# The FFN's down projection as seven-product block multiplications

## The chip, the cores and the metric

The kernel runs on one core of one Trainium2 chip. The metric is the device time of one execution in microseconds (us). The five engines are called as in the profile: PE (matrix multiply; PEld is its weight load), DVE (vector), ACT (scalar), POOL (GpSimd) and SP (which here only issues DMA transfers).

## What is computed

One layer of an encoder for 1024 prompt tokens and 64 sample tokens, 1088 in all, with 1024 channels. The change lies in its last part, the SwiGLU feed-forward network (FFN) with 2816 hidden channels:

```
xn2 = rms_norm(x, lw["norm_ffn_g"])
f = (jax.nn.silu(xn2 @ lw["w_ffn_gate"]) * (xn2 @ lw["w_ffn_up"])) @ lw["w_ffn_down"]
x = x + f
```

The products before it (attention, a recurrent branch, memory attention, three branch projections, one output projection) are not changed.

## The kernel before

**Numbers in two parts.** Every matrix operand is split into a high part (a cast on ACT, line 72) and a low part (a subtraction on DVE, line 73). A product is three matmuls: high by high, high by low, low by high. Activations lie with channels on the 128 partitions and the 1088 tokens along the free dimension, so a "block" of 128 channels is a 128 x 1088 tile.

**The plain form.** `down` (line 1210 and on) takes one block of 128 output channels at a time. For each of three token chunks (364, 364, 360) it accumulates over the contraction blocks of a group, three matmuls each (`mm3`, lines 101 to 103), into one PSUM bank; DVE then adds the bank to the output tile (line 1229). The 22 hidden blocks are taken in groups of 8, 8 and 6, and within each group all 8 output blocks: 24 calls.

**The seven-product form.** The branch projections, the output projection, gate and up already use `sw_product` (line 202). It takes a pair of output blocks at a time and pairs of contraction blocks, and the tokens in two halves of 544, so that each pair is a 2 x 2 by 2 x 2 block product, done with seven products in place of eight. `PAIRS` (line 168) lists the seven with their operands in the order in which PE does them: A11, S3, S2, A22, S1, A12, S4 on the weight side and B11, T3, T2, T4, T1, B21, B22 on the activation side. For each of the seven PE does two column pieces of 272, and for each piece all contraction pairs, three matmuls each (line 212). The first three products are copied out of PSUM by ACT (line 218), because later results need them as well; the others are evacuated by the caller's `out` on DVE and POOL.

`sw_weights` (line 170) loads the weights of one such step (two transfers of 512 KB on SP), forms the four combinations S1 to S4 on DVE and splits all seven operands on ACT and DVE. The steps run one ahead: while PE does one, the next one's weights are made. For the branch outputs the activation side comes from DRAM: `put_branch` (line 293) stores three blocks as they are, forms T3, T1, T2, T4 on POOL in place (lines 299 to 302) and stores those; `load_operands` (line 996) loads 28 operands of 272 KB, seven for each of four contraction pairs, and splits each into the place from `operand_at` (line 993). A place is free once PE has done the earlier product with the operand that lies there.

**Gate, up and down.** For each of 11 pairs of hidden blocks, `gate_pair` and `up_pair` do a gate and an up step. The results are scaled per token on POOL (line 1169), gate goes through SiLU on ACT (line 1178), and DVE multiplies them (line 1185). `up_pair` then stores the two hidden blocks whole to DRAM (`hid_scr`, line 1187). For the down projection `load_h` (line 1203) loads them back, 544 KB each, in the order of need, and splits them. The down weights come through `load_w` on ACT's DMA queue. The last group's finished output blocks are transposed on PE (line 1244), copied by ACT (line 1246) and written out, while the next block is being computed.

A scheduler of the framework puts the instructions of each engine in order when the kernel is built. Each engine, and SP's queue, then works in that order, and an instruction that waits holds up all behind it on its engine.

Of the kernel before, what the change touches and what calls it, by code (L numbers as in the profile page):

```python
# [9 lines left out]
F32 = mybir.dt.float32  # L10
# [39 lines left out]
def kernel(ctx: ExitStack, tc: tile.TileContext, x_prompt, x_sample, mem_prompt, cache_sb_k, cache_sb_v,  # L50
# [16 lines left out]
    def f32(t):  # L67
        return t.bitcast(F32)

    def split(h, l, src, h_eng=None, l_eng=None):  # L70

        (h_eng or S.copy)(h, src)  # L72
        (l_eng or V).tensor_sub(l, src, f32(h))  # L73
# [216 lines left out]
    o_scr = [{o: [drm.tile([P, HT], F32, name=f"o{b}{o}{i}") for i in range(KT // 2)] for _, o in PAIRS}  # L290
             for b in range(3)]

    def put_branch(b, i, x0, x1):

        d = o_scr[b]
        x0l, x0h, x1l, x1h = x0[:, :HT], x0[:, HT:], x1[:, :HT], x1[:, HT:]
        for o, src in (("B22", x1h), ("B11", x0l), ("B21", x1l)):
            ST.dma_start(d[o][i], src)
        G.tensor_sub(x1h, x1h, x0h)
        G.tensor_sub(x0h, x0h, x0l)  # L300
        G.tensor_add(x0l, x0l, x1h)
        G.tensor_sub(x1l, x1l, x0l)
        for o, src in (("T3", x1h), ("T1", x0h), ("T2", x0l), ("T4", x1l)):
            ST.dma_start(d[o][i], src)

    def o_tile(name):
        return wpl.tile([P, T], F32, tag="wx", name=name, bufs=3)
# [629 lines left out]
    if True:  # L937
# [4 lines left out]
        NI = KT // 2  # L942
        LO, HI = slice(0, HT), slice(HT, T)
        x1_scr = [drm.tile([P, T], F32, name=f"x1_{k}") for k in range(KT)]
        hid_scr = [drm.tile([P, T], F32, name=f"hid{k}") for k in range(FFN // P)]


        UNITS = [(act, f"A{x}{k}") for k in range(KT) for x in "hl"] + [(bp, f"B{k}") for k in range(16)]
# [3 lines left out]
        def at(place, name, dt=F32R):  # L952
            return place[0].tile([P, T], dt, tag=place[1], name=name, bufs=RAWB if place is RAW else 1)
# [19 lines left out]
        def pair_weights(src, j, nm):  # L973
            return sw_weights(src[0, :, 2 * j * P:2 * (j + 1) * P], f"{nm}{j}", w_slot, w_stage)
# [21 lines left out]
        def load_operands(b):  # L996
            X = {o: [] for _, o in PAIRS}
            for oi, (_, o) in enumerate(PAIRS):
                for i in range(NI):
                    t = operand_at(oi, i, f"x{b}{o}{i}")  # L1000
                    ST.dma_start(f32(t[:, 1]), o_scr[b][o][i])
                    split(t[:, 0], t[:, 1], f32(t[:, 1]))
                    X[o].append(t)
            return X

        def form_operands(xs, temps, nm):

# [44 lines left out]

        br_w = (w_br_sb, w_br_lru, w_br_mem)
        W = pair_weights(w_br_sb, 0, "wb0")
        X = load_operands(0)
        for b in range(3):
            for j in range(NI):
                if j + 1 < NI:
                    Wn = pair_weights(br_w[b], j + 1, f"wb{b}")
                elif b < 2:  # L1060
                    Wn = pair_weights(br_w[b + 1], 0, f"wb{b + 1}")
                else:
                    Wn = pair_weights(w_out, 0, "wo")
                branch_pair(b, j, W, X)
                W = Wn
            if b < 2:
                X = load_operands(b + 1)
# [114 lines left out]
        def up_pair(j, W, sil):  # L1182
            u = [at(cycle("u", U_PLACES), f"u{j}{f}", F32) for f in range(2)]
            sw_product(W, XS, NI, banks4, temp,
                       ffn_out(u, lambda f, hf, c, d: V.tensor_mul(d, d, sil[f][:, piece(hf, c)])))  # L1185
            for f in range(2):
                ST.dma_start(hid_scr[2 * j + f], u[f])

        for j in range(NH // 2):
            Wn = pair_weights(w_ffn_up, j, "fu")  # L1190
            sil = gate_pair(j, W)
            W = pair_weights(w_ffn_gate, j + 1, "fg") if j + 1 < NH // 2 else None
            up_pair(j, Wn, sil)


        groups = [list(range(0, 8)), list(range(8, 16)), list(range(16, 22))]
        Hh, Hl = {}, {}

        def load_h(j):
            q = 2 * (j % 16)  # L1200
            Hh[j] = at(UNITS[q], f"hh{j}")
            Hl[j] = at(UNITS[q + 1], f"hl{j}")
            ST.dma_start(f32(Hl[j]), hid_scr[j])
            split(Hh[j], Hl[j], f32(Hl[j]))

        def load_x1(f):
            mg[f] = mgp.tile([P, T], F32, tag=f"mg{f}", name=f"y{f}")
            ST.dma_start(mg[f], x1_scr[f])
# [11 lines left out]
        for j in groups[0]:  # L1220
            load_h(j)
        mg = [None] * KT
        load_x1(0)
        for gi, js in enumerate(groups):
            fin = gi == len(groups) - 1
            Xg = ([Hh[j] for j in js], [Hl[j] for j in js])
            for f in range(KT):
                def ev(s, n, p):
                    V.tensor_add(mg[f][:, s:s + n], mg[f][:, s:s + n], p)  # L1229

                if gi == 0:
                    load_h(8 + f)
                    if f + 1 < KT:
                        load_x1(f + 1)
                w = load_w(w_ffn_down[0, js[0] * P:(js[-1] + 1) * P, f * P:(f + 1) * P], f"fd{gi}{f}", nk=len(js))
                down(w, Xg, ev, len(js))
                if fin:
                    for g in range(3):
                        m = 4 if g < 2 else 1
                        n = P if g < 2 else DSEQ  # L1240
                        p = ps.tile([P, 512], F32, tag="tr", name="ytp", bufs=2)
                        for q in range(m):
                            t = 4 * g + q
                            TE.transpose(p[:n, q * P:(q + 1) * P], mg[f][:, t * P:t * P + n], ident)  # L1244
                        yt = at(SPARE[g], "yt", F32)
                        S.copy(yt[:n, :m * P], p[:n, :m * P])
                        fs = slice(f * P, (f + 1) * P)
                        if g < 2:
                            ST.dma_start(y_prompt[0, g * 512:(g + 1) * 512, fs].rearrange("(t p) n -> p t n", p=P),
                                              yt[:, :512].rearrange("p (t n) -> p t n", n=P))  # L1250
                        else:
                            ST.dma_start(y_sample[0, :, fs], yt[:n, :P])
            if gi == 0:
                for j in groups[2]:
                    load_h(j)
# [32 lines left out]
```

## Time and profile before

| what | us |
|---|---|
| median of 3 runs (2421.33 to 2422.0) | 2421.39 |
| the profiled execution's own time | 2413.88 |
| its span, first to last instruction | 2412.1 |
| PE busy in the span | 2324.9 |
| DVE busy | 1346.5 |
| ACT busy | 1027.7 |
| POOL busy | 623.8 |
| mean granted PE clock, share of full | 0.989 |

The spans below are counted from the first instruction. Gate and up run from about 1650 to 2127, the down projection from there to the end. In the timeline a row merges instructions of one kind: its start, the time that it covers, the engine, the line, the tiles written and read, a count, and in brackets the idle time before it and what ended it. A matmul's own duration includes the flow through the array, so the distance between starts says what one costs in a stream.

### The profile page before, as it was taken

How to read it: one execution, taken by the hardware profiler on the slowest of the kernel's cores; microseconds unless marked ns; L12 is line 12 of the kernel's file. 1: busy time of each engine (PE TensorE's matmuls, PEld its weight loads, DVE VectorE, ACT ScalarE, POOL GpSimd, SP SyncE). 2: the span in 40 equal slices, each digit the busy share in tenths (PEclk: the TensorE clock that was granted, in tenths of full speed). 3: DMA queues.
4: the chain of work that ended last, by engine and by line, in shares of the span. 5: the costliest groups of instructions: out<-in, count | busy, mean ns of one | idle time of the engine just before them, and what ended most of it. 6: DMA issues, size and time to landing. Idle time of an engine off the chain costs nothing.

```text
span 2412.1 us, 39508 instructions
## 1 busy us (share of the span) xinstructions
PE 2324.9 (96%) x15941; PEld 2271.5 (94%) x15941; DVE 1346.5 (56%) x2248; ACT 1027.7 (43%) x1968; POOL 623.8 (26%) x657
## 2 busy tenths in 40 slices
PE   7999999999999999999999999798999999999999
PEld 6899999989999999999998998698999999989998
DVE  4666666665555554334466876769565656562322
ACT  5555555553534533323354653465433343330211
POOL 3223232321222221111113365624322222210000
PEclk9999999999999999999999999898999999999999
DMA  4112121213233233222255662142222222261222
GB/s 145 56 51 69 51 76 52 76 56 109 81 118 105 81 121 106 83 96 90 83 189 174 215 231 91 54 156 85 77 83 72 83 71 90 77 242 59 83 58 63
DMA packets 254221, 238.87 MB, mean 99 GB/s; under 512 B 11331, under 2 KB 217366, under 8 KB 254038
## 3 DMA queue, kind: packets, MB, share of 16 engines
q1 hardware_dynamic: 132184, 172.30, 21.3%
q10 hardware_dynamic: 121854, 64.05, 9.1%
q8 instruction: 125, 2.05, 0.4%
q14 instruction: 58, 0.48, 0.1%
HBM read 167.32 MB, written 68.98 MB: 98 GB/s over the span
## 4 chain that ended last, share of the span: by engine, by line
PE 64%; POOL 5%; DVE 3%; issue 2%; DMA 2%; ACT 2%; SPq 0%; ACTq 0%; POOLq 0%; DVEq 0%
PE sw L212 24%; PE mm L103 11%; PE mm L101 11%; PE mm L102 11%; POOL swt L1045 2%; POOL mg L1049 2%; DMA sig<-g 1%; PE mmk L101 1%; PE mmk L102 1%; PE mmk L103 1%; PE ytp L1244 0%; DVE xgT L73 0%; PE gt L103 0%; PE gt L101 0%; PE gt L102 0%
## 5 line engine op out<-in xcount | busy, mean ns | idle before, releaser
L218 ACT COPY swt<-sw 128x272 f32<-128x272 f32 x228 | 86.8, 386 | 137.2 <-PE sw L212 132.1
L1229 DVE TENSOR_TENSOR y<-y,mm 128x364 f32<-128x364 f32 (+1 forms) x72 | 38.3, 531 | 181.6 <-PE mm L103 181.6
L1169 POOL TENSOR_TENSOR u<-u,R 128x272 f32<-128x272 f32 x66 | 66.5, 1009 | 180.8 <-DVE u L1168 180.8
L460 DVE TENSOR_TENSOR_SCAN e<-ones,e 128x128 f32<-128x128 f32 (+3 forms) x64 | 97.0, 1525 | 0.8
L277 DVE TENSOR_SCALAR gst<-mm,prm 128x364 f32<-128x364 f32 (+1 forms) x72 | 42.6, 592 | 98.3 <-PE mm L103 98.0
L1169 POOL TENSOR_TENSOR sil<-sil,R 128x272 f32<-128x272 f32 x66 | 51.2, 779 | 140.8 <-DVE sil L1168 139.3
L459 DVE SCALAR_TENSOR_TENSOR e<-z,e 128x384 f32<-128x384 f32 (+4 forms) x96 | 50.4, 552 | 61.2 <-ACT e L457 57.6
L464 ACT ACTIVATE e<-e 128x128 f32<-128x128 f32 (+3 forms) x64 | 43.8, 685 | 60.0 <-DVE e L463 52.2
L1185 DVE TENSOR_TENSOR u<-u,sil 128x272 f32<-128x272 f32 x88 | 40.3, 461 | 47.2 <-POOL u L1169 46.5
L1045 POOL TENSOR_TENSOR swt<-swt,sig 128x272 f32<-128x272 f32 x48 | 49.2, 1024 | 66.3 <-DVE swt L1044 45.7
L1178 ACT ACTIVATE sil<-sil 128x272 f32<-128x272 f32 x88 | 37.5, 431 | 61.9 <-POOL sil L1169 57.2
L73 DVE TENSOR_TENSOR al<-at,ah 128x128 fp32r<-128x128 f32 (+2 forms) x96 | 51.1, 547 | 20.5 <-ACT ah L72 20.5
L1049 POOL TENSOR_TENSOR mg<-mg,swt 128x272 f32<-128x272 f32 x64 | 60.6, 956 | 5.5 <-DVE swt L1047 1.8
L748 POOL TENSOR_TENSOR ig<-ig,xc 128x1092 f32<-128x1092 f32 x8 | 20.4, 2554 | 129.2 <-ACT ig L740 129.2
L1038 ACT ACTIVATE sig<-sig 128x544 f32<-128x544 f32 x48 | 31.3, 662 | 50.7 <-DMA sig<-g 40.9
L101 PE MATMUL z<-kh,qh 128*128 128x384 f32 (+4 forms) x96 | 36.6, 381 | 14.6 <-DVE e L463 14.6
L455 ACT ACTIVATE e<-z 128x384 f32<-128x384 f32 (+4 forms) x96 | 45.7, 484 | 10.6 <-PE z L103 7.7
L463 DVE TENSOR_TENSOR e<-z,e 128x384 f32<-128x384 f32 (+4 forms) x96 | 48.9, 542 | 0.0
L820 POOL TENSOR_TENSOR sq<-sq,sqt 128x364 f32<-128x364 f32 (+1 forms) x12 | 13.6, 1131 | 133.1 <-ACT sqt L819 133.1
L72 ACT CAST ah<-at 128x128 fp32r<-128x128 f32 (+2 forms) x96 | 43.0, 471 | 10.1 <-PE at L512 10.1
L102 PE MATMUL av<-al,vh 128*128 128x256 f32 x160 | 46.7, 292 | 0.2
L101 PE MATMUL av<-ah,vh 128*128 128x256 f32 x160 | 46.4, 290 | 0.4 <-ACT ah L72 0.4
(1813 smaller groups left out, 8492.2 us busy)
## 6 DMA issues: line engine op xcount, KB each, us to landing
sig<-g SPq DMA_DIRECT2D x48, 272.0 KB
hid<-u SPq DMA_DIRECT2D x22, 544.0 KB
hl<-hid SPq DMA_DIRECT2D x22, 544.0 KB
g<-gst SPq DMA_DIRECT2D x48, 182.0 KB
out_dram<-kvs SPq DMA_DIRECT2D x32, 256.0 KB
o0T<-oh SPq DMA_DIRECT2D x16, 272.0 KB
o1T<-ol SPq DMA_DIRECT2D x16, 272.0 KB
o2T<-om SPq DMA_DIRECT2D x16, 272.0 KB
```

The source lines that it names most:

```text
L73: (l_eng or V).tensor_sub(l, src, f32(h))
L101: TE.matmul(out, lh, rh, start=start, stop=False)
L102: TE.matmul(out, lh, rl, start=False, stop=False)
L103: TE.matmul(out, ll, rh, start=False, stop=stop)
L212: TE.matmul(bank[c][:, :HC], w[:, wj, i], x[:, xj, cs], start=start and i == 0 and j == 0, stop=i == n - 1 and j == 2, skip_group_check=True)
L218: S.copy(tmp[c][:, j], bank[c][:, :HC])
L459: V.scalar_tensor_tensor(ev, z, 0.0, ev, op0=ALU.max, op1=ALU.add)
L460: V.tensor_tensor_scan(e[:, ::-1], ones1[:n].to_broadcast([n, L]), e[:, ::-1], 0.0, op0=ALU.mult, op1=ALU.add)
L463: V.tensor_sub(ev, z, ev)
L1045: G.tensor_mul(t if b else d, t, g)
L1049: G.tensor_add(d, d, t)
L1169: G.tensor_mul(d, d, r)
```

## The change

`up_pair` no longer stores the hidden blocks whole. It calls `put_operands`, which is the body of `put_branch` with the destination given, so that each pair leaves seven block operands of 272 KB in DRAM. `load_operands` takes a list of such sets. The down projection runs through `sw_weights`, `load_operands` and `sw_product` in 12 steps: three groups of 4, 4 and 3 contraction pairs, four pairs of output blocks in each. At each group's beginning 28 (at the last 21) operands are loaded into the places that the step before is still using. The first step's weights are made during the last up step, and all down weights now come on SP's queue. DVE evacuates each step with two additions in place of one where a kept product is needed; for the last pair of output blocks the second is on POOL. In the last group, the outputs of a step are transposed and written after the next step is issued, with their copies in the pool that also holds the kept products (`raw`, three buffers).

```diff
-    def put_branch(b, i, x0, x1):
-
-        d = o_scr[b]
+    def put_operands(d, x0, x1):
+
         x0l, x0h, x1l, x1h = x0[:, :HT], x0[:, HT:], x1[:, :HT], x1[:, HT:]
         for o, src in (("B22", x1h), ("B11", x0l), ("B21", x1l)):
-            ST.dma_start(d[o][i], src)
+            ST.dma_start(d[o], src)
         G.tensor_sub(x1h, x1h, x0h)
         G.tensor_sub(x0h, x0h, x0l)
         G.tensor_add(x0l, x0l, x1h)
         G.tensor_sub(x1l, x1l, x0l)
         for o, src in (("T3", x1h), ("T1", x0h), ("T2", x0l), ("T4", x1l)):
-            ST.dma_start(d[o][i], src)
+            ST.dma_start(d[o], src)
...
-        hid_scr = [drm.tile([P, T], F32, name=f"hid{k}") for k in range(FFN // P)]
+        h_scr = [{o: drm.tile([P, HT], F32, name=f"h{o}{i}") for _, o in PAIRS} for i in range(FFN // P // 2)]
...
-            for f in range(2):
-                ST.dma_start(hid_scr[2 * j + f], u[f])
+            put_operands(h_scr[j], *u)
+
+        groups = [range(0, 4), range(4, 8), range(8, 11)]
...
-            W = pair_weights(w_ffn_gate, j + 1, "fg") if j + 1 < NH // 2 else None
+            W = pair_weights(w_ffn_gate, j + 1, "fg") if j + 1 < NH // 2 else down_weights(0, 0)
...
-        def down(w, X, evac, nk):
-            wh, wl = w
-            for ci, (s, n) in enumerate(CH):
-                pool, tag = BANKS[ci]
-                p = pool.tile([P, 512], F32, tag=tag, name="mm", bufs=2)
-                for k in range(nk):
-                    mm3(p[:, :n], wh[:, k, :], wl[:, k, :], X[0][k][:, s:s + n], X[1][k][:, s:s + n],
-                        k == 0, k == nk - 1)
-                evac(s, n, p[:, :n])
...
+        def down_pair(gi, j, W, X):
+            def out(f, hf, c, p, t, add):
+                d = mg[2 * j + f][:, piece(hf, c)]
+                if add:
+                    V.tensor_add(t, p, t)
+                    (G if j == NI - 1 else V).tensor_add(d, d, t)
+                else:
+                    V.tensor_add(d, d, p)
...
+            sw_product(W, X, len(groups[gi]), banks4, temp, out)
...
-                        yt = at(SPARE[g], "yt", F32)
+                yt = at(RAW, "yt", F32) if g < 2 else half("yt")
...
+        for q, (gi, j) in enumerate(steps):
+            if j == 0:
+                X = load_operands([h_scr[i] for i in groups[gi]], f"h{gi}")
+            Wn = down_weights(*steps[q + 1]) if q + 1 < len(steps) else None
+            down_pair(gi, j, W, X)
+            W = Wn
+            if gi == len(groups) - 1 and j > 0:
+                y_out(2 * j - 2)
+                y_out(2 * j - 1)
+        y_out(KT - 2)
+        y_out(KT - 1)
```

On POOL, between one up step and the next gate step, before (`u` is a hidden block, `sil` the gate's result, `R` the token scale):

```order
L1169 TENSOR_TENSOR u_20439<-u_20439,R_17275 128x272 x2
L1169 TENSOR_TENSOR sil_20679<-sil_20679,R_17275 128x272 x2
L1169 TENSOR_TENSOR sil_20679<-sil_20679,R_17276 128x272 x2
L1169 TENSOR_TENSOR sil_20678<-sil_20678,R_17275 128x272 x2
L1169 TENSOR_TENSOR u_20916<-u_20916,R_17275 128x272 x2
```

And on POOL at the same place now:

```order
L1176 TENSOR_TENSOR u_20548<-u_20548,R_17330 128x272 x2
L298 TENSOR_TENSOR u_20549<-u_20549,u_20548 128x544
L299 TENSOR_TENSOR u_20548<-u_20548 128x544
L300 TENSOR_TENSOR u_20548<-u_20548,u_20549 128x544
L301 TENSOR_TENSOR u_20549<-u_20549,u_20548 128x544
L1176 TENSOR_TENSOR sil_20797<-sil_20797,R_17330 128x272 x2
```

The four combinations stand between the up step's last scaling and the next gate step's first.

On SP, where the last up step passes into the down projection, before (`hl` is a hidden block loaded back, `y<-x` an output tile preset with the residual):

```order
L1203 DMA hl_22563<-hid_12603 128x1088
L1203 DMA hl_22654<-hid_12604 128x1088
L1187 DMA hid_12616<-u_22313 128x1088
L1203 DMA hl_22745<-hid_12605 128x1088
L1203 DMA hl_22836<-hid_12606 128x1088
L1187 DMA hid_12615<-u_22312 128x1088
L1203 DMA hl_22927<-hid_12607 128x1088
L1208 DMA y_22931<-x_5_12592 128x1088
```

And on SP at the same place now (`h0B`, `h0T` are the first group's operands; `hB`, `hT` on the left are the last pair's stores):

```order
L1005 DMA h0B_22789<-hB_12607 128x544
L1005 DMA h0B_22793<-hB_12614 128x544
L303 DMA hT_12666<-u_22489 128x544
L303 DMA hT_12669<-u_22488 128x544
L303 DMA hT_12667<-u_22488 128x544
L303 DMA hT_12668<-u_22489 128x544
L1005 DMA h0B_22797<-hB_12621 128x544
L1005 DMA h0B_22801<-hB_12601 128x544
L1005 DMA h0B_22805<-hB_12608 128x544
L1005 DMA h0B_22809<-hB_12615 128x544
L1005 DMA h0B_22813<-hB_12622 128x544
L177 DMA fd01r_22817<-in_w_ffn_down_dram 128x4x256
```

Before, two stores stand among the loads there; now the last five loads of the first group (the last B21 and all four B22) stand behind the last pair's four T stores, which wait for POOL.

On DVE, where the first down step begins to be evacuated, before (`fd` are down weights, the last letter h or l the part):

```order
L73 TENSOR_TENSOR hl_23109<-hl_23109,hh_23108 128x1088
L73 TENSOR_TENSOR fd02l<-fd02r,fd02h 128x1024
L73 TENSOR_TENSOR hl_23200<-hl_23200,hh_23199 128x1088
L1229 TENSOR_TENSOR y_22567<-y_22567,mm 128x364 x2
L1229 TENSOR_TENSOR y_22567<-y_22567,mm 128x360
L73 TENSOR_TENSOR fd03l<-fd03r,fd03h 128x1024
L1229 TENSOR_TENSOR y_22658<-y_22658,mm 128x364 x2
```

And on DVE at that place now (`sw` is PSUM, `swt` a kept product):

```order
L1214 TENSOR_TENSOR swt<-sw,swt 128x272
L73 TENSOR_TENSOR h0B_22797<-h0B_22797 128x544
L1214 TENSOR_TENSOR swt<-sw,swt 128x272
L73 TENSOR_TENSOR h0B_22801<-h0B_22801 128x544
L1214 TENSOR_TENSOR swt<-sw,swt 128x272
L1215 TENSOR_TENSOR y_22850<-y_22850,swt 128x272 x2
L73 TENSOR_TENSOR h0B_22805<-h0B_22805 128x544
L1214 TENSOR_TENSOR swt<-sw,swt 128x272
L73 TENSOR_TENSOR h0B_22809<-h0B_22809 128x544
L1215 TENSOR_TENSOR y_22850<-y_22850,swt 128x272
L1214 TENSOR_TENSOR swt<-sw,swt 128x272
L73 TENSOR_TENSOR h0B_22813<-h0B_22813 128x544
```

The splits of the last loads stand between the evacuations of the first step, and each holds up those behind it.

More of the change, by code (lines that the diff above doesn't have):

```diff
@@ L303, in put_branch @@
         for o, src in (("T3", x1h), ("T1", x0h), ("T2", x0l), ("T4", x1l)):
-            ST.dma_start(d[o][i], src)
+            ST.dma_start(d[o], src)
+    def put_branch(b, i, x0, x1):
+        put_operands({o: o_scr[b][o][i] for _, o in PAIRS}, x0, x1)
     def o_tile(name):
@@ L994, in operand_at, with load_operands @@
             return at(UNITS[oi * NI + i], name).rearrange("p (x n) -> p x n", x=2)
-        def load_operands(b):
+        def load_operands(srcs, nm):
             X = {o: [] for _, o in PAIRS}
             for oi, (_, o) in enumerate(PAIRS):
-                for i in range(NI):
-                    t = operand_at(oi, i, f"x{b}{o}{i}")
-                    ST.dma_start(f32(t[:, 1]), o_scr[b][o][i])
+                for i, d in enumerate(srcs):
+                    t = operand_at(oi, i, f"{nm}{o}{i}")
+                    ST.dma_start(f32(t[:, 1]), d[o])
                     split(t[:, 0], t[:, 1], f32(t[:, 1]))
@@ L1004, in load_operands, with load_branch @@
             return X
+        def load_branch(b):
+            return load_operands([{o: o_scr[b][o][i] for _, o in PAIRS} for i in range(NI)], f"x{b}")
         def form_operands(xs, temps, nm):
@@ L1054 @@
         W = pair_weights(w_br_sb, 0, "wb0")
-        X = load_operands(0)
+        X = load_branch(0)
         for b in range(3):
@@ L1066 @@
             if b < 2:
-                X = load_operands(b + 1)
+                X = load_branch(b + 1)
         tt = [at(p, "tt", F32).rearrange("p (x n) -> p x n", x=2) for p in (RAW, SPARE[3])]
@@ L1185, in up_pair, with down_weights @@
                        ffn_out(u, lambda f, hf, c, d: V.tensor_mul(d, d, sil[f][:, piece(hf, c)])))
-            for f in range(2):
-                ST.dma_start(hid_scr[2 * j + f], u[f])
+            put_operands(h_scr[j], *u)
+        groups = [range(0, 4), range(4, 8), range(8, 11)]
+        mg = [None] * KT
+        def down_weights(gi, j):
+            r = groups[gi]
+            return sw_weights(w_ffn_down[0, 2 * r[0] * P:2 * (r[-1] + 1) * P, 2 * j * P:2 * (j + 1) * P],
+                              f"fd{gi}{j}", w_slot, w_stage)
         for j in range(NH // 2):
@@ L1191 @@
             sil = gate_pair(j, W)
-            W = pair_weights(w_ffn_gate, j + 1, "fg") if j + 1 < NH // 2 else None
+            W = pair_weights(w_ffn_gate, j + 1, "fg") if j + 1 < NH // 2 else down_weights(0, 0)
             up_pair(j, Wn, sil)
[L1196 to L1204, printed above, removed]
@@ L1206, in load_x1 @@
-        def load_x1(f):
-            mg[f] = mgp.tile([P, T], F32, tag=f"mg{f}", name=f"y{f}")
-            ST.dma_start(mg[f], x1_scr[f])
-        def down(w, X, evac, nk):
-            wh, wl = w
-            for ci, (s, n) in enumerate(CH):
-                pool, tag = BANKS[ci]
-                p = pool.tile([P, 512], F32, tag=tag, name="mm", bufs=2)
-                for k in range(nk):
-                    mm3(p[:, :n], wh[:, k, :], wl[:, k, :], X[0][k][:, s:s + n], X[1][k][:, s:s + n],
-                        k == 0, k == nk - 1)
-                evac(s, n, p[:, :n])
@@ L1220 @@
[L1220 to L1244, printed above, removed]
-                        yt = at(SPARE[g], "yt", F32)
[L1246 to L1252, printed above, removed]
-            if gi == 0:
-                for j in groups[2]:
-                    load_h(j)
@@ new lines, in down_pair @@
+        def down_pair(gi, j, W, X):
[6 more added lines that the diff above has]
+                    V.tensor_add(d, d, p)
+            if gi == 0:
+                for k in (2 * j, 2 * j + 1):
+                    mg[k] = mgp.tile([P, T], F32, tag=f"mg{k}", name=f"y{k}")
+                    ST.dma_start(mg[k], x1_scr[k])
+            sw_product(W, X, len(groups[gi]), banks4, temp, out)
@@ new lines, in y_out @@
+        def y_out(f):
+            for g in range(3):
+                m = 4 if g < 2 else 1
+                n = P if g < 2 else DSEQ
+                p = ps.tile([P, 512], F32, tag="tr", name="ytp", bufs=2)
+                for q in range(m):
+                    t = 4 * g + q
+                    TE.transpose(p[:n, q * P:(q + 1) * P], mg[f][:, t * P:t * P + n], ident)
+                yt = at(RAW, "yt", F32) if g < 2 else half("yt")
+                S.copy(yt[:n, :m * P], p[:n, :m * P])
+                fs = slice(f * P, (f + 1) * P)
+                if g < 2:
+                    ST.dma_start(y_prompt[0, g * 512:(g + 1) * 512, fs].rearrange("(t p) n -> p t n", p=P),
+                                 yt[:, :512].rearrange("p (t n) -> p t n", n=P))
+                else:
+                    ST.dma_start(y_sample[0, :, fs], yt[:n, :P])
@@ new lines @@
+        steps = [(gi, j) for gi in range(len(groups)) for j in range(NI)]
+        for q, (gi, j) in enumerate(steps):
[9 more added lines that the diff above has]
+        y_out(KT - 1)
```

## The prediction

> **What bounds the kernel now.** I began with the page's first part, then looked at the two stages in the table of windows (columns: stretch, its length, busy time and instructions of PE, PEld, DVE, ACT, POOL, then the granted clock, the DMA engines' busy share and GB/s).
>
> ```profile
> PE 2324.9 (96%) x15941; PEld 2271.5 (94%) x15941; DVE 1346.5 (56%) x2248; ACT 1027.7 (43%) x1968; POOL 623.8 (26%) x657
> 1686.00:2112.00 426.00, 424.64 (x3399) 424.00 (x3398) 249.60 (x473) 162.80 (x352) 112.87 (x127) 1.00 0.25 80
> 2112.00:2133.00 21.00, 17.17 (x127) 16.56 (x126) 19.12 (x26) 13.07 (x15) 6.79 (x6) 0.95 0.96 335
> 2126.90:2412.10 285.20, 275.77 (x1658) 272.21 (x1656) 87.24 (x119) 47.30 (x62) 0.88 (x1) 0.99 0.27 87
> ```
>
> PE bounds both stages. In gate and up it has 1.4 us of 426 free; in the down projection (last row) DVE is busy for 87 of 285 us and POOL hardly at all. Only between them is PE not the bound: from 2112 to 2133 the DMA engines are 0.96 busy and DVE 19.1 of 21 us. So the change is worth what it takes from PE, less what the joints then cost. The timeline of PE gives the rates and the joint:
>
> ```profile
> 2105.94 3.15 PE L212 MATMUL sw<-xgB,fu10A 128*128 128x272 f32 x24
> ...
> 2123.92 3.15 PE L212 MATMUL sw<-xgB,fu10S 128*128 128x272 f32 x24
> 2130.90 0.67 PE L101 MATMUL mm<-hh,fd00h 128*128 128x364 f32 x1 [3.83 <-ACT fd00h L72]
> ...
> 2302.78 0.33 PE L101 MATMUL mm<-hh,fd16h 128*128 128x364 f32 x1
> ...
> 2314.76 0.33 PE L101 MATMUL mm<-hh,fd17h 128*128 128x364 f32 x1
> ```
>
> Seven-product form: six groups of 24 matmuls of 272 columns lie between 2105.94 and 2123.92, so one costs 17.98/144 = 124.9 ns. The last up step ends at 2123.92 + 24 x 0.125 = 2126.9. Plain form: a call with 8 blocks is 8 x 3 x 3 = 72 matmuls in 2314.76 - 2302.78 = 11.98, or 166.4 ns each. Per column that is 0.459 ns in both (a plain matmul has 362.7 columns on average), so the smaller matmul costs nothing extra.
>
> **The sum before,** from 2126.9 to the end at 2412.1: 285.2 us.
>
> ```profile
> 2335.67 0.71 PE L1244 MATMUL ytp<-ident,y 128*128 128x128 f32 x5
> ...
> 2396.51 0.71 PE L1244 MATMUL ytp<-ident,y 128*128 128x128 f32 x5
> ...
> 2406.56 1.62 PE L1244 MATMUL ytp<-ident,y 128*128 128x128 f32 x9
> 2407.24 1.47 ACT L1246 COPY yt<-ytp 128x512 f32<-128x512 f32 x3 [8.58 <-PE ytp L1244]
> 2409.05 0.53 SPq L1252 DMA_DIRECT2D out_dram<-yt  x1
> SPq L1284 <- DMA out_dram<-yt: 1.4, 1, 1.4
> L1246 ACT COPY yt<-ytp x24: 257/582/589, 2336.4 to 2408.5; 128x512 f32<-128x512 f32 x16, 64x128 f32<-64x128 f32 x8
> ```
>
> - Matmuls: 22 blocks x 8 outputs x 9 = 1584, at 166.4 ns: 263.6.
> - Transposes: six outputs lie between the first two rows, 60.84/6 = 10.14 each, of which 54 matmuls are 9.0; so 1.15 an output, 8.0 for the seven beside which PE goes on.
> - The tail, from the last transposes at 2406.56: 5.5.
> - The rest, 8.1, is the joint: the wait of 3.83 for the first weights, shorter ones and a slow clock behind it.
>
> **The sum after.**
>
> *Matmuls.* 11 contraction pairs x 4 output pairs x 7 products x 2 pieces x 3 = 1848, which is also what the built order holds, at 124.9 ns: 230.8. That is 32.8 less. *Transposes beside PE's work:* four outputs, 4.6.
>
> *The tail.* Now four outputs, not one, are transposed behind the last step: eight large copies through three `raw` buffers, each free when its transfer has landed. The trace has no such chain. A small transfer lands at 2409.05 + 0.53 + 1.4 = 2410.98, 1.9 after its issue; a load of twice the size of mine takes, in the rows quoted for the first joint below, 3.8 from its issue. I take 2.7. A round is then a copy (0.58) and a landing, 3.3. First copy after 0.7, two rounds, 0.9 to the second buffer of the third, 3.3 again, and 1.1 as now from the last landing to the end: 12.6. If the chain didn't bind, eight copies and a landing would be 9; with 3.8 landings it is 16.
>
> *Within gate and up.* POOL gets four combinations of 544 columns per pair, and seven stores take the place of two.
>
> ```profile
> 1928.46 0.77 POOL L1169 TENSOR_TENSOR sil<-sil,R 128x272 f32<-128x272 f32 x1 [10.61 <-DVE sil L1168]
> 1919.54 0.44 DVE L1185 TENSOR_TENSOR u<-u,sil 128x272 f32<-128x272 f32 x1
> L302 POOL TENSOR_TENSOR om<-om,om x4: 1362/1966/2221, 1069.8 to 1270.8; 128x544 f32<-128x544 f32 x4
> 1927.99 6.59 SPq L177 DMA_DIRECT2D fg7r<-in_w_ffn_gate_dram  x2
> ```
>
> The hidden block is done at 1919.54 + 0.44 = 1919.98 and POOL next wanted at 1928.46: 8.5 free. The same four combinations exist already for the branches; one took 1.36 to 2.22, so four are 5.4 to 8.9, nearly always inside the gap. The T stores go out within it too, and the weight loads behind them on SP go out at 1927.99 anyway. I put 0.5 on the whole stage; nothing, or 0.4 a pair (4), are the ends. Cover gone means: SiLU on ACT late, and behind it weight casts and kept copies.
>
> *The first joint.* The loads of the first group start as places come free in the last up step, six of seven products (18 us) ahead of need. What limits them is DVE. For its rates I use the change from the first branch to the second, where the same 28 operands are split under the same code:
>
> ```profile
> 1331.35:1371.80 40.45, 40.17 (x321) 39.95 (x320) 39.98 (x63) 28.69 (x55) 16.66 (x14) 1.00 0.68 242
> 1335.63 0.69 DVE L194 TENSOR_TENSOR wb10s<-wb10r,wb10r 128x512 f32<-128x512 f32 x1
> 1336.23 0.69 DVE L197 TENSOR_TENSOR wb10s<-wb10r,wb10s 128x512 f32<-128x512 f32 x1
> 1352.43 3.26 DVE L73 TENSOR_TENSOR x1T<-x1T 128x544 fp32r<-128x544 f32 x5
> 1371.76 0.77 DVE L1047 TENSOR_TENSOR swt<-sw,sig 128x272 f32<-128x272 f32 x2
> 2108.38 13.05 SPq L1203 DMA_DIRECT2D hl<-hid  x10
> 2112.15 1.10 ACT L72 CAST hh<-hl 128x1088 fp32r<-128x1088 f32 x1 [1.12 <-DMA hl<-hid]
> ```
>
> In a stream, a weight row of 512 costs DVE 0.60 from start to start, an operand of 544 (3.26 - 0.72)/4 = 0.635, an evacuation of 272 about 0.35. In the changed order DVE does 28, 13 and 25 of these from the first operand to the last B22: 34.5 us. It can start at about 2112 (the row shows the first operand's cast there now). POOL slows it: in the window of 40.45, the 63 instructions are 28 operands, 20 weight rows and 15 evacuations, 35.0 by these rates; DVE was busy for 39.98, so 5.0 was lost beside 16.7 of POOL. Beside the six scalings and four combinations at this joint, some 12 us, that is 3.6. The last B22 is then split at 2150. PE, unhindered, wants it at 2126.9 + 18 + 1 = 2146: 4 late, and I add 1 for the clock: 5. The last five loads behind the T stores, which wait for POOL until about 2138, come to about the same. Bounds: 0 (DVE keeps up) and 12.
>
> The shared engine port bears on this: by the Trainium skill's "SBUF — State Buffer", section "SBUF: two separate sides", a DVE instruction with two SBUF inputs and a POOL instruction exclude one another for the whole instruction. By that rule the 12 us of POOL would all be added to DVE's time, the joint would cost about 13, and the kernel end at 2401. The window agrees that there is a price, but not on its size: 5.0 lost beside 16.7.
>
> *The two group changes.* The branches' changes, three steps each:
>
> ```profile
> 1347.52 3.17 PE L212 MATMUL sw<-x1B,wb10A 128*128 128x272 f32 x24
> ...
> 1415.69 3.17 PE L212 MATMUL sw<-x1B,wb13A 128*128 128x272 f32 x24
> ...
> 1436.74 3.17 PE L212 MATMUL sw<-x2B,wb20A 128*128 128x272 f32 x24
> ...
> 1508.51 3.17 PE L212 MATMUL sw<-x2B,wb23A 128*128 128x272 f32 x24
> ```
>
> Three steps of 168 matmuls are 62.9. The changes lost 5.3 and 8.9. Much of that was the gates of the branches (their loads ahead of ACT's copies, two POOL multiplications per piece), which the down projection lacks; DVE has six more evacuations a step instead. I take 1.5 and, for the smaller last group, 1. Ends: 0 and 8.9 each. For PE waiting on copies among the last group's transposes, 1 (0 to 3).
>
> Sum: 230.8 + 4.6 + 12.6 + 0.5 + 5 + 1.5 + 1 + 1 = 257.0, which is 28.2 less than 285.2. The span goes from 2412.1 to 2383.9, the profiled execution from 2413.88 to 2385.7. The median of the runs lies 7.5 above the profiled time, and is forecast at 2421.39 - 28.2 = 2393.2.
>
> **The rivals.**
>
> *Joints as dear as the dearest.* In-order DVE and ACT stall PE at each change as between the second and third branch: 8.9 twice, 12 at the first joint: +22.3, or 2415.5. For it: DVE is then busy nearly throughout, as in the window of 40.45. Against: that window itself lost PE only 0.3 us (40.17 busy).
>
> *No joint binds.* Joints and the stage cost nothing and the tail is 9: 244.4, 40.8 less: 2380.6. For it: the same window. Against: the first joint's DVE sum.
>
> *Gate and up become POOL's (slower than before).* Place: POOL between the last scaling of an up step and the first of the next gate step, in all 11 pairs. If the four combinations outlast 8.5 us, ACT's SiLU, then casts, DVE and PE fall behind. It decides the sign where a pair loses 28.2/11 = 2.6, that is where four take over 11 (2.8 each), plus what slack ACT and DVE have. At 3.5 each, 5.5 a pair is lost: +60, less 28: 2453. The longest in the row quoted is 2.22, so it has little for it.
>
> *A fixed price per matmul.* If a matmul cost the same for its weight load whatever its columns, 264 more would lose. At the full 166.4 for each, 1848 are 307.5, and the kernel ends at 2421.39 - 28.2 + 76.7 = 2470. The two equal prices per column speak against it.
>
> The Trainium skill's "TensorE: Matmul & The Clock Gate", section "Back-to-back issue gap", gives such a rule: with weight loads in the stream about 81 ns at 128 columns and 131 at 512. Interpolated, an estimate, that is 100 at 272 and 112 at 363, and the seven-product form would lose 7 us on PE (184 against 177). The trace has 124.9 and 166.4, and does not agree.
>
> That the change doesn't do what it says is out: the built order holds 1848 matmuls for 1584.
>
> **How the numbers follow.** Forecast 68%, dear joints 13%, no joint 13%, POOL 3%, fixed price 1%, and 2% for something between the dear joints and no change. All but the last three are faster by more than 0.2%, or 4.8 us, which is about what a measurement of this kernel can tell: 0.94, with 0.02 for same and 0.04 for slower. The range reaches from nearly the case without joints, 2382, to 2407, most of the way to the dear ones.
>
> **What would show it.** Right: matmuls of line 212 at 125 ns through the down projection; PE's gaps at its first step's last products, named after DVE or ACT; a span from last up step to end of about 257. Wrong: POOL waits in place of its gaps in gate and up, a distance between gate steps over 42 us, or gaps of several us at each group's first step.

## The result and the profile after

| | before | after |
|---|---|---|
| median of the runs, us | 2421.36 (2413.38 to 2422.0) | 2386.84 (2383.01 to 2390.25) |
| profiled execution, us | 2413.88 | 2384.59 |
| span, us | 2412.1 | 2382.8 |
| from the last up step's end to the end, us | 285.2 | 256.4 |

The ratio is 0.9868, with a 95% interval of 0.9852 to 0.9885. The forecast was 2393.2 (2382 to 2407), and 257.0 for the last row. First, the table of windows of the changed kernel (columns as in the prediction): the first down step, the first step of the second group, and the tail.

```profile
2126.40:2154.80 28.40, 24.12 (x170) 22.82 (x169) 27.42 (x45) 11.25 (x23) 8.34 (x6) 0.94 0.70 237
2217.90:2239.00 21.10, 21.10 (x171) 21.10 (x170) 21.10 (x40) 10.75 (x22) 1.19 (x1) 1.00 0.36 127
2371.00:2382.80 11.80, 5.70 (x39) 3.91 (x37) 0.44 (x1) 5.21 (x12) 0.00 (x0) 0.94 0.63 189
```

PE lost most in two places, the first step (24.1 of 28.4 busy, DVE busy for 27.4) and the tail. In the second group's first step DVE was busy for all of 21.1 us and PE lost nothing. The timeline of PE shows it step by step:

```profile
2126.42 3.17 PE L212 MATMUL sw<-h0B,fd00A 128*128 128x272 f32 x24
...
2154.80 3.17 PE L212 MATMUL sw<-h0B,fd01A 128*128 128x272 f32 x24
2157.81 6.18 PE L212 MATMUL sw<-h0T,fd01S 128*128 128x272 f32 x48
...
2217.94 3.17 PE L212 MATMUL sw<-h1B,fd10A 128*128 128x272 f32 x24
...
2238.99 3.17 PE L212 MATMUL sw<-h1B,fd11A 128*128 128x272 f32 x24
...
2302.13 2.42 PE L212 MATMUL sw<-h2B,fd20A 128*128 128x272 f32 x18
...
2316.72 2.52 PE L212 MATMUL sw<-h2B,fd20S 128*128 128x272 f32 x18 [0.72 <-DVE swt L1214]
2319.08 2.42 PE L212 MATMUL sw<-h2B,fd21A 128*128 128x272 f32 x18
...
2353.00 1.04 PE L1232 MATMUL ytp<-ident,y 128*128 128x128 f32 x8
...
2371.14 1.04 PE L1232 MATMUL ytp<-ident,y 128*128 128x128 f32 x8
```

24 matmuls take 2157.81 - 2154.80 = 3.01 us, 125.3 ns each; a step of 168 is 21.05, one of 126 is 15.79. The first step took 28.38, 7.3 too long. The next three and the first of the second group are 21.05 each. The first of the third group took 16.95, 1.2 too long. A step with the transposes of two outputs took 18.14, 2.35 more than 15.79. The tail is 2382.8 - 2371.14 = 11.66.

PE's waits in the first step:

```profile
2134.33 0.64 PE L212 MATMUL sw<-h0T,fd00S 128*128 128x272 f32 x3 [0.88 <-DVE h0T L73]
2136.12 2.01 PE L212 MATMUL sw<-h0T,fd00S 128*128 128x272 f32 x14 [1.14 <-DVE h0T L73]
2139.71 0.64 PE L212 MATMUL sw<-h0T,fd00A 128*128 128x272 f32 x3 [1.07 <-DVE h0T L73]
...
2152.96 2.01 PE L212 MATMUL sw<-h0B,fd00S 128*128 128x272 f32 x14 [0.59 <-DVE h0B L73]
```

They are waits for DVE's splits. Of the 7.3 us, 5.8 are lost in the second to fourth product (2129.43 to 2144.27, 14.84 for 72 matmuls that take 9.02), 0.7 in the fifth, where the granted clock is down to 0.80, and 0.8 in the last. What DVE and POOL did then:

```profile
2132.41 7.25 DVE L73 TENSOR_TENSOR h0T<-h0T 128x544 fp32r<-128x544 f32 x4
...
2140.18 2.62 DVE L73 TENSOR_TENSOR h0T<-h0T 128x544 fp32r<-128x544 f32 x4
```

```profile
2131.97 1.73 POOL L298 TENSOR_TENSOR u<-u,u 128x544 f32<-128x544 f32 x1 [3.19 <-DVE u L1192]
...
2137.36 1.71 POOL L301 TENSOR_TENSOR u<-u,u 128x544 f32<-128x544 f32 x1
```

Four splits took 7.25 us beside POOL's four combinations, and 2.62 once these were done. DVE lost 4.6 us there.

### The profile page after: what moved, and what is told of

It is laid out like the page before. It is cut to its first block, busy times and chain, and to the rows that moved or that the text cites. A ratio compares the mean times of both kernels' runs of the same rounds, so it can differ in the third digit from the quotient of the medians.

```text
span 2382.8 us, 40913 instructions
## 1 busy us (share of the span) xinstructions
PE 2295.9 (96%) x16205; PEld 2241.8 (94%) x16205; DVE 1473.9 (62%) x2489; ACT 1089.7 (46%) x2155; POOL 718.1 (30%) x719
## 4 chain that ended last, share of the span: by engine, by line
PE 63%; DVE 4%; POOL 4%; issue 2%; DMA 2%; ACT 2%; SPq 0%; ACTq 0%; POOLq 0%; DVEq 0%
PE sw L212 34%; PE mm L101 7%; PE mm L103 7%; PE mm L102 7%; POOL swt L1052 2%; POOL mg L1056 1%; DMA sig<-g 1%; PE mmk L101 1%; PE mmk L102 1%; PE mmk L103 1%; DMA x0B<-o0B 1%; DVE h0T L73 0%; DVE xgT L73 0%; PE gt L103 0%; PE gt L101 0%
## 5 line engine op out<-in xcount | busy, mean ns | idle before, releaser
L218 ACT COPY swt<-sw 128x272 f32<-128x272 f32 x300 | 113.8, 385 | 159.7 <-PE sw L212 153.6
L1215 POOL TENSOR_TENSOR y<-y,swt 128x272 f32<-128x272 f32 x18 | 19.4, 1088 | 212.0 <-DVE swt L1214 212.0
L457 ACT ACTIVATE e<-z 128x384 f32<-128x384 f32 (+4 forms) x96 | 45.7, 484 | 10.6 <-PE z L103 7.7
```

Of the source, the lines that this page charges most:

```text
L218: S.copy(tmp[c][:, j], bank[c][:, :HC])
```

## The experiments

My theory after this: the first joint is DVE's, and most of its loss is the price of POOL's combinations running beside it (*port*). The rivals: the loads that stand behind the T stores on SP (*queue*), and DVE's waits for POOL's scalings of the last up step.

The times of one kernel differ by some us from run to run, and so does, in the traces, the time at which gate and up begin (1647 to 1658 us); from there on the pairs of gate and up behind the first agree to 0.05 us, but for the one kernel that changes them. So beside the medians I compare two lengths of the trace: the first down step, and the stretch from the last up step's end to the end.

| kernel | first step | stretch | median |
|---|---|---|---|
| changed kernel | 28.38 | 256.4 | 2386.84 |
| combinations behind the first step | 27.60 | 255.2 | 2387.88 |
| T stores behind the loads | 28.29 | 254.9 | 2387.63 |
| combinations on DVE | 23.53 (overlaps the second) | 253.7 | 2384.51 |
| seven places for copies | 28.48 | 255.1 | 2389.91 |
| combinations on DVE, later | 23.84 | 251.3 | 2383.27 |
| the same with seven places | 23.69 | 252.6 | 2383.23 |
| the same with groups 3, 4, 4 | 19.41 | 252.6 | 2382.93 |
| groups 3, 4, 4 alone | 28.59 | 261.6 | 2394.51 |
| the same, T stores behind the loads | 24.82 | 256.4 | 2387.39 |
| eight POOL instructions a pair | 29.23 | 257.1 | 2413.99 |

With groups 3, 4, 4 a first step of 126 matmuls is 15.79 unhindered, else 21.05.

### The last pair's combinations behind the first step

```diff
-            put_operands(h_scr[j], *u)
+            if j + 1 < NH // 2:
+                put_operands(h_scr[j], *u)
+            else:
+                last_u.append((j, u))
...
             down_pair(gi, j, W, X)
             W = Wn
+            if last_u:
+                jl, ul = last_u.pop()
+                put_operands(h_scr[jl], *ul)
```

> The last pair's four POOL combinations, and the stores of its block operands, are moved behind the first step of the down projection. Theory (port): DVE is slowed while POOL combines, 4 splits of 544 columns taking 7.25 us in place of 2.5. Without the combinations the first step falls from 28.4 us to 23 to 25 and the kernel from 2386.8 to about 2382. Rival (order): DVE waits in its own order for POOL's scalings of the last up step, whatever the combinations do; then the first step stays above 27 us and the time within 1.5 us. Either way the combinations now lie beside the second step, where DVE has 16 of 63 us free, and cost nothing there.

The combinations did not go where I sent them: POOL has nothing else to do there, and began as soon as the three stores had landed, still in the first step. DVE's rows in this kernel, then POOL's:

```profile
2134.15 2.62 DVE L73 TENSOR_TENSOR h0T<-h0T 128x544 fp32r<-128x544 f32 x4
...
2146.29 1.84 DVE L73 TENSOR_TENSOR h0B<-h0B 128x544 fp32r<-128x544 f32 x1
2148.06 0.43 DVE L1218 TENSOR_TENSOR swt<-sw,swt 128x272 f32<-128x272 f32 x1
2139.68 4.60 POOL L298 TENSOR_TENSOR u<-u,u 128x544 f32<-128x544 f32 x1 [9.16 <-DMA hB<-u]
```

The first four h0T splits are back at 2.62 for four, and PE no longer waits there; the slowing moved with POOL to the h0B splits, about 9 us later in the step, and PE waited 2.62 for those. The step fell by 0.8 only. So the slowing goes where POOL goes, but the saving that I expected did not come, because the edit did not take POOL out of the step.

### The T stores behind the loads

```diff
-            ST.dma_start(d[o], src)
+            if late is None:
+                ST.dma_start(d[o], src)
+            else:
+                late.append((d[o], src))
...
             down_pair(gi, j, W, X)
             W = Wn
+            for o, src in late:
+                ST.dma_start(o, src)
+            late.clear()
```

> The combinations stay where they are; only the last pair's four T stores, which wait for them on SP, are issued behind the first group's loads. Theory (port): the loads that stand behind the T stores come about 6 us earlier, but DVE is as slow as before: the first step keeps 27 to 28.4 us, the time within 1 us of 2386.8. Rival (queue): the five late loads are what PE waits for; the first step falls to 24 to 25 us, the time by 3 to 4 us.

```profile
2133.16 4.64 SPq L1008 DMA_DIRECT2D h0B<-hB  x8
```

In the changed kernel the last five loads were issued from 2139.51 - 2126.42 = 13.1 us into the first step on. Here they are the last five of the eight in this row, which goes from 3.2 to 7.8 us into it. The step took 28.29, and four splits again 7.24. With these groups the queue is not the cause. The stretch is 1.5 shorter mostly because the third group's first step took 15.89 this time.

### The combinations on DVE

```diff
-        G.tensor_sub(x1h, x1h, x0h)
+        E.tensor_sub(x1h, x1h, x0h)
...
-            put_operands(h_scr[j], *u)
+            put_operands(h_scr[j], *u, eng=V if j + 1 == NH // 2 else G)
```

> The last pair's four combinations run on DVE in place of POOL. Theory (port): DVE gets 4 x 0.7 = 2.8 us more work and loses the 4.7 us of slowing: the first step falls by 1 to 3 us, to about 26.5. Rival (DVE is slow there for another reason, as DMA traffic at 0.7): its work grows by 2.8 us and the first step grows to 30 to 31 us.

Here the scheduler let the second step begin before the first was over, so the two are taken together: 47.57 us against 49.43, a gain of 1.9. That is in the range of the theory; the rival had the step grow. DVE with four more instructions was done sooner than DVE beside POOL with four fewer. All seven stores and the loads are still there, and DVE's splits behind the last combination run at full rate, so the transfers don't slow them:

```profile
2145.64 2.62 DVE L73 TENSOR_TENSOR h0T<-h0T 128x544 fp32r<-128x544 f32 x4
```

### The combinations on DVE, behind the first step

```diff
             down_pair(gi, j, W, X)
             W = Wn
+            if q == 1:
+                jl, ul = last_u.pop()
+                put_operands(h_scr[jl], *ul, eng=V)
```

> The last pair's combinations run on DVE, and behind the first step of the down projection (they stand among the second step's work), its stores with them. Nothing runs on POOL in the first step then. Theory (port): the first step loses 2 to 3.5 us in place of 7.4 (DVE's waits for the scalings and the slow clock stay), 23 to 24.5 us in all, the second step nothing. Rival (the first step is bound by loads or by the waits for scalings): it stays above 26 us.

In the program they now stand behind the second step, and the scheduler put them early into it. Rows of PE and then of DVE:

```profile
2132.34 3.17 PE L212 MATMUL sw<-h0B,fd00A 128*128 128x272 f32 x24
...
2154.33 2.01 PE L212 MATMUL sw<-h0B,fd00S 128*128 128x272 f32 x14 [0.69 <-DVE h0B L73]
2156.18 3.17 PE L212 MATMUL sw<-h0B,fd01A 128*128 128x272 f32 x24
2138.40 2.62 DVE L73 TENSOR_TENSOR h0T<-h0T 128x544 fp32r<-128x544 f32 x4
2161.97 0.71 DVE L299 TENSOR_TENSOR u<-u,u 128x544 f32<-128x544 f32 x1
```

The step took 23.84, inside the theory's range, 28.38 - 23.84 = 4.5 us less. The edit takes POOL's four combinations out of it and the seven stores with them. That the 4.5 us are the combinations' and not the stores' follows from two other numbers: DVE's four splits alone lost 4.6 beside POOL, and with the stores in place but nothing on POOL the splits ran at full rate. The other 2.8 stay, 2.0 of them in the last product: short waits for DVE's splits, the longest 0.69. In the second step, where the combinations are now, PE lost nothing.

### Groups of 3, 4 and 4

```diff
-        groups = [range(0, 4), range(4, 8), range(8, 11)]
+        groups = [range(0, 3), range(3, 7), range(7, 11)]
```

> The changed kernel with its three groups of 3, 4 and 4 contraction pairs in place of 4, 4 and 3. The first step then has 126 matmuls (15.8 us), 21 operands and weight rows three quarters as long. Theory (DVE's list of work sets what the first joint loses, and POOL beside it adds 4.5 whatever the group): DVE's list is 6 to 7 us shorter and PE wants its last operand 4.5 us sooner, so the joint loses 1.5 to 2.5 less than 7.4: a first step of 20.7 to 21.7 us, and about 254.5 us from the last up step to the end in place of 256.4. Rival (the loss belongs to the waits for the last up step's outputs, not to the operands): the joint keeps 7.4, a first step of 23.2.

Both theories missed: the step of 15.8 us took 28.6. PE, ACT, DVE and SP at its end, and POOL's first combination:

```profile
2161.48 4.45 PE L212 MATMUL sw<-h0B,fd00S 128*128 128x272 f32 x18 [7.12 <-DVE swt L1214]
2159.97 0.51 ACT L72 CAST fd01A<-fd01r 128x384 fp32r<-128x384 f32 x1 [10.60 <-DMA fd01r<-in_w_ffn_down_dram]
2160.52 0.56 DVE L73 TENSOR_TENSOR fd01A<-fd01r,fd01A 128x384 fp32r<-128x384 f32 x1 [4.33 <-ACT fd01A L72]
2160.99 0.43 DVE L1214 TENSOR_TENSOR swt<-sw,swt 128x272 f32<-128x272 f32 x1
2149.71 5.54 SPq L303 DMA_DIRECT2D hT<-u  x4
2155.34 0.98 SPq L177 DMA_DIRECT2D fd01r<-in_w_ffn_down_dram  x2
2143.62 6.06 POOL L298 TENSOR_TENSOR u<-u,u 128x544 f32<-128x544 f32 x1 [3.06 <-DVE u L1192]
```

Read from the bottom: POOL's first combination took 6.06, so the T stores went out from 2149.71 on, and the second step's weights behind them at 2155.34. ACT waited 10.6 for these, DVE 4.3 for ACT, and behind that split in DVE's order stood the evacuation for whose PSUM bank PE waited 7.12. The queue, which cost nothing with four pairs, seems to be a large part here. To test that:

> Groups of 3, 4 and 4 as in the run before, and the last pair's four T stores issued behind the second step's weight loads, which stood behind them on SP. The combinations stay on POOL in the first step. Theory (queue: the 7.12 us that PE waited there were those loads, held by stores that wait for POOL): the wait goes, the first step falls from 28.6 us to 20.5 to 23, and the stretch from the last up step to the end from 261.6 to 254 to 256 us. Rival (port: POOL's combinations slow DVE as much with three pairs): the first step stays above 26 us.

```profile
2150.35 4.05 PE L212 MATMUL sw<-h0B,fd00S 128*128 128x272 f32 x18 [2.25 <-DVE swt L1218]
2135.87 0.91 SPq L177 DMA_DIRECT2D fd01r<-in_w_ffn_down_dram  x2
2138.37 5.54 SPq L1254 DMA_DIRECT2D hT<-u  x4
2136.58 1.76 POOL L298 TENSOR_TENSOR u<-u,u 128x544 f32<-128x544 f32 x1 [3.06 <-DVE u L1195]
2136.42 4.30 DVE L73 TENSOR_TENSOR h0T<-h0T 128x544 fp32r<-128x544 f32 x3
```

The wait of 7.12 fell to 2.25, the step by 3.8, to 24.82, and the stretch by 5.2, to 256.4. The step lies between the two expectations. The late loads were most of that one wait, but not of the step: of the 12.8 us that it lost, 9.0 stay. And the edit is not the only difference between the two traces: POOL's first combination took 6.06 before and 1.76 here, so the T stores could go out 3.6 us sooner in the step (8.95 against 12.57) whatever stands before them. How much of the 3.8 is the edit's is not separated. Of the 9.0, PE spent 3.2 in three waits for ACT's copies (1.10, 0.65, 1.49), which stand in ACT's order behind casts that wait for loads of B operands; POOL beside DVE is there as well (three splits in 4.30). That three pairs make the joint cheaper did not come true in either.

### Later combinations, seven places for the output copies, both, and all three

```diff
-                yt = at(RAW, "yt", F32) if g < 2 else half("yt")
+                yt = at(cycle("y", Y_PLACES), "yt", F32) if g < 2 else half("yt")
```

`Y_PLACES` are seven of the `h` operand places that the last group doesn't use.

> The large output copies go to seven free places in place of three raw buffers, so no copy waits for a transfer to land. Theory (the chain of the prediction): the tail behind the last step falls from 11.7 us to about 9, the time by 2 to 3 us. Rival (the chain hardly binds; the waits shown for landings are 0.4 + 0.55 + 0.16 us, and copies and transposes follow one another anyhow): by 0 to 1.1 us.

ACT in the tail of the changed kernel, and then with seven places:

```profile
2376.72 0.74 ACT L1234 COPY yt<-ytp 64x128 f32<-64x128 f32 x2 [0.39 <-DMA out_dram<-yt]
2378.01 0.58 ACT L1234 COPY yt<-ytp 128x512 f32<-128x512 f32 x1 [0.55 <-DMA out_dram<-yt]
2378.76 0.74 ACT L1234 COPY yt<-ytp 128x512 f32<-128x512 f32 x2 [0.16 <-DMA out_dram<-yt]
```

```profile
2388.09 1.23 ACT L1237 COPY yt<-ytp 128x512 f32<-128x512 f32 x3 [0.63 <-PE ytp L1235]
2389.73 0.54 SPq L1243 DMA_DIRECT2D out_dram<-yt  x1
```

The waits for landings are gone and the tail is 2392.8 - 2381.89 = 10.91, 0.75 less: the rival. What is left is copies and transposes in turn (1.85 an output) and 2.5 from the last issue to the end. The two edits together:

> The late combinations on DVE together with the seven places for the output copies. Theory (the two are independent): from the last up step to the end 251.3 - 0.75 = 250.5 us, where the changed kernel has 256.4 and the kernel before 285.2, and a median of some 2382. Rival (the shorter tail came from the schedule of that one run): 251.3.

252.6, not 250.5. The first step kept its gain and the tail fell by 0.3 only; the first steps of the second and third group took 0.8 and 1.8 us longer than unhindered. Over all the kernels with four pairs first, these two changes lost 0 to 0.8 and 0.1 to 1.8 us, without any edit there; why is open.

> Late combinations on DVE, seven places for the output copies, and groups of 3, 4 and 4. Theory (DVE's list): without POOL beside it the joint lost 2.8 us with four pairs; with three it loses 0.3 to 1.3, a first step of 16.1 to 17.1 us; the second group's operands are then split while DVE also combines, which has room. From the last up step to the end 248 to 249 us. Rival (the loss lies in waits for the last up step's outputs): 250.5, a first step of 18.6.

19.41 and 252.6: both are above the two expectations, and nearer to the rival's. Before its last product PE waits 2.19 for an evacuation on DVE, then goes on slowly (3.5 us for 18 matmuls, at a granted clock of 0.63). None of the three versions is faster than another by more than the runs differ, and against the changed kernel the gain of some 3.6 us in the median (ratio to before 0.9851, 0.9836 to 0.9865, for the late combinations alone) lies within the two intervals; only the traces' 3.8 to 5.1 us show it, one trace each, and 0.9 of the 5.1 is the third group's first step, which no edit touched.

### The price of a smaller matmul, alone

The kernel before, its plain form in four chunks of 272:

```diff
-            for ci, (s, n) in enumerate(CH):
+            for ci in range(4):
+                s, n = ci * HC, HC
```

> The kernel before, its plain down projection cut into four pieces of 272 columns in place of three of 362 or 363: 2112 matmuls in place of 1584, the same columns, seven stores and combinations absent. Theory (the price goes by columns, 0.459 ns each): 2112 x 124.9 ns = 263.8 us against 263.6, so the stretch from the last up step to the end stays 285 us, within 2. Rival (each matmul carries a fixed price): at 166.4 ns each the stretch is longer by 528 x 166.4 ns = 88 us. By the Trainium skill, TensorE: Matmul & The Clock Gate, section Back-to-back issue gap, an estimate of 100 ns at 272 columns and 112 at 363 would make it longer by 34 us.

The median is 2419.43 against 2417.92, ratio 1.0001 (0.999 to 1.0012). The third and fourth call begin at:

```profile
2164.13 0.28 PE L101 MATMUL mm<-hh,fd02h 128*128 128x272 f32 x1
2176.15 0.28 PE L101 MATMUL mm<-hh,fd03h 128*128 128x272 f32 x1
```

96 matmuls in 12.02 us are 125.2 ns each, where 72 of 363 columns took 11.98. At these two widths the price goes by columns. The stretch is 288.1, 2.9 longer, which the expectation missed by 0.9: some 1.3 in the joint, 0.05 in each call with eight blocks behind it, and 1.2 in the last group before the last call.

### The stores alone

The kernel before, with `put_operands` called for each pair in addition to its own stores.

> The kernel before with one part of the change alone: every pair also makes the four combinations and stores its seven block operands; the plain down projection stays and reads what it read. Theory: in gate and up the combinations lie in POOL's gap and a pair stays at 41.95 us; at the joint the weights and inputs of the plain form are split on DVE beside the last combinations, so the joint grows by 0 to 3 us and the time by as much. Rival (the stores and combinations cost something in each pair): 0.4 a pair, 4 us over the stage, seen as a pair of 42.3.

A pair of gate and up steps stayed at 41.95 us. The stretch grew from 285.2 to 290.0, above the expected 0 to 3, all in the joint; the median by the ratio 1.002 (1.0009 to 1.0032). So the plain form, too, would have paid for the combinations and stores at that place, 4.8 us. PE waited 4.3 and 5.8 us for weights in place of 3.8 and 1.6, and the longer wait ends with a cast on ACT that itself waited 6.9 us for its load; so there a transfer came last, not DVE. How much of it the stores or POOL caused is not separated. POOL there, while DVE waits for ACT:

```profile
2144.55 1.35 POOL L313 TENSOR_TENSOR u<-u,u 128x544 f32<-128x544 f32 x1
```

Alone, a combination takes 1.35; beside DVE in the changed kernel they follow one another at 1.79.

### Twice the work for POOL in gate and up

```diff
+        if twice:
+            for h in (x1l, x0h):
+                G.tensor_add(h, h, x0l)
+                G.tensor_sub(h, h, x0l)
```

> The changed kernel with eight POOL instructions of 544 columns in place of four in each of the first ten pairs (an addition and the subtraction that undoes it, twice). They take about 14.1 us, beyond the 8.5 of POOL's gap. By the prediction's threshold (what outlasts the gap is lost): 5.6 us a pair, +56 us. Rival (POOL late by 4 us at the next gate step is still early enough, since its product is wanted only in the up step that follows; POOL would be busy for 25 of 42 us): a pair stays within 0.3 us of 41.95 and the time within 3 us.

Neither: a pair took 43.97, 2.0 more (the first 3.9 more). One gate step, PE's row and then the chain that leads to it, in order of time:

```profile
1954.05 3.27 PE L212 MATMUL sw<-xgB,fg6S 128*128 128x272 f32 x24 [1.73 <-DVE sil L1179]
1948.16 1.84 DVE L73 TENSOR_TENSOR fu6A<-fu6r,fu6A 128x512 fp32r<-128x512 f32 x1
1949.93 0.77 DVE L1179 TENSOR_TENSOR sil<-sw,swt 128x272 f32<-128x272 f32 x2
1951.18 1.49 POOL L1180 TENSOR_TENSOR sil<-sil,R 128x272 f32<-128x272 f32 x2
1951.98 0.43 ACT L1189 ACTIVATE sil<-sil 128x272 f32<-128x272 f32 x1 [7.72 <-POOL sil L1180]
1952.95 0.69 DVE L73 TENSOR_TENSOR fu6S<-fu6s,fu6S 128x512 fp32r<-128x512 f32 x1 [2.25 <-ACT fu6S L72]
```

POOL holds up DVE's weight operands, one for one (six at 1.74 to 1.85), so the gate's first evacuation comes 15.8 us into the step, where the changed kernel has it at 12.4. POOL, still at the last of its eight, adds some 0.7, and its scaling comes 4.1 later than there. From here it is the chain of the prediction's rival: ACT's SiLU waits for the scaling, the cast behind it is late, DVE's split waits 2.25 for the cast, and PE 1.73 for the evacuation behind that split. So of the 4.1 us, 3.4 are DVE's, and only the rest is the lateness of POOL itself, which the rival had as the start. About half of the 4.1 was slack. In the changed kernel, too, DVE is held up beside the four (three instructions at 1.74 to 1.85 in place of 0.60), and PE has no such wait.

## Why the prediction was right, step by step

- *Matmuls*, 230.8: 1848 x 125.3 ns = 231.5. The rival with a fixed price is refuted by the four chunks alone. So is, for these two widths, the rule of the Trainium skill's "TensorE: Matmul & The Clock Gate", section "Back-to-back issue gap", by which the four chunks would have been 34 us slower, as the expectation estimated.
- *Gate and up*, 0.5: nothing; the last ten pairs took 419.5 us in both kernels. The cover was right. The threshold of the POOL rival was not: with the work doubled a pair lost 2.0, where what outlasts the gap was 5.6. Its chain (SiLU, casts, DVE, PE) was then seen, but mostly started by DVE's slowed weight rows and not by POOL's gap.
- *The first joint*, 5: 7.3. The mechanism, DVE beside POOL, was right, its size not: "5.0 lost beside 16.7" gave 0.30 us of DVE lost per us of POOL, and it was 4.5 beside 7.1, 0.63. The window of the prediction was no measure for this: its POOL instructions have 272 columns, not 544, and among DVE's instructions there are evacuations from PSUM, which POOL does not slow. Without POOL's combinations the joint lost 2.8, where the prediction's list (34.5 us from 2112, wanted at 2146) and 1 for the clock give 1.5. The list is a little off: the trace has 28, 11 and 25 instructions there, not 28, 13 and 25, 33.1 us by the same rates, and it lacks 3.0 us in which DVE stood idle for the scalings of the last up step. From the first split at 2111.05 to the end of the last, 41.8 us, these are 33.1 + 3.0 + 4.6 beside POOL, and 1.1 over. The place was wrong too: PE was to wait at the last products and lost 5.8 of the 7.3 us from the second to the fourth. The second reason, that the loads behind the T stores "come to about the same", failed: moving the stores changed nothing. With three pairs what stood behind them and was late were the second step's weights, not these loads.
- The page "SBUF — State Buffer" of the Trainium skill, section "SBUF: two separate sides", whose exclusion the prediction found too strong by its window, describes these rows better than my rate: where the two meet, they alternate whole instructions, 1.79 us for each pair. Its sum, an estimate, failed all the same: the four combinations cost DVE 4.6 us, not their whole length and the scalings' besides; the joint lost 7.3, not 13.
- *Group changes*, 1.5 and 1: 0 and 1.2, and *the transposes' hiccups*, 1: 2 x 2.35 - 4.6 = 0.1. DVE fully busy was no loss for PE, as the rival "no joint binds" had said of these places; nothing speaks for the rival "as dear as the dearest" (8.9 each).
- *The tail*, 12.6: 11.7. The chain of buffers hardly binds, only 0.75 of it.
- Sum: 231.5 + 7.3 + 0 + 1.2 + 4.7 + 11.7 = 256.4, against 257.0. Terms that were 3.2 too low and 3.8 too high in all cancelled; that the sum is within 0.6 is luck in part.
- *The offset*, 7.5 between the profiled execution and the median: 2.3 after. It was treated as a constant, and is chance: 25 runs of the kernel before lay between 2412.3 and 2424.8, with a median of 2417.92. This alone is 5.3 of the 6.4 us by which the forecast was too high, and it is most of the reason why the medians differ by 34.5 us where the stretch became only 28.8 shorter.

## What to carry to other kernels

Where a chain of DVE instructions with two SBUF inputs sets the pace, look at what POOL does in that very stretch and move it to where DVE has room, or do it on DVE; and test by where it then runs, since an idle engine starts as soon as it may, whatever its place in the program. A store that costs nothing in a queue under one size of group can hold up the loads behind it under another. Price a step from the rows of that step, and an offset from several executions.

## What the runs showed of the hardware

DVE and POOL alternated, one whole instruction each, where both read two operands from SBUF: from start to start a split of 544 columns took 1.79 us in place of 0.635, and a combination 1.79, where one alone took 1.35. DVE's evacuations that read PSUM did not slow: 0.43 with POOL at work. And POOL could be held out for long: its first combination took 4.60 and 6.06 us in two kernels, with DVE's stream at full speed meanwhile. If the work itself takes 1.35, an estimate from the row alone, POOL got in at 2142.9 in the one, where DVE read PSUM, and at 2148.3 in the other, just before DVE stood idle for 0.38 us; but in the changed kernel it got in almost at once. Which of the two yields at the start of such a stretch is not settled.
